# Sample value products of a decoder step with the probabilities stationary in column groups, and their rows turned by PE

## The chip, the cores and the metric

The kernel runs on one core of one Trainium2 chip. The metric is the device time of one execution in microseconds. It was timed three times; the figure used is the median. One more execution was taken with the hardware profiler, and every duration below is from it.

## The reference

One inference step of a hybrid decoder layer: 512 prompt tokens and, beside them, 8 sequences with 4 new tokens each (32 sample rows). The model width is 1024, all inputs are float32. What matters here is the sliding-window attention of the sample rows: 8 query heads over 2 key/value heads of 128 columns, a window of 128 cached keys per sequence, and the 4 new keys of the sequence itself.

```python
    qg = qb.reshape(B, N, Tq, N_KV, G, HD)
    s = jnp.einsum('bnqkgd,bnskd->bnkgqs', qg, kb).astype(jnp.float32) * (HD ** -0.5)
    ...
    s = jnp.where(valid[None, :, None, None], s + bias, -jnp.inf)
    sk = sink.astype(jnp.float32).reshape(1, 1, N_KV, G, 1, 1)
    m = jnp.maximum(jnp.max(s, axis=-1, keepdims=True), sk)
    p = jnp.exp(s - m)
    p = p / (jnp.sum(p, axis=-1, keepdims=True) + jnp.exp(sk - m))
    o = jnp.einsum('bnkgqs,bnskd->bnqkgd', p.astype(vb.dtype), vb)
    ...
        kk = jnp.concatenate([k_cache.astype(k.dtype), k], axis=1)
        vv = jnp.concatenate([v_cache.astype(v.dtype), v], axis=1)
```

The last `einsum`, probabilities times values, is the value product. Its result goes through an output projection (`w_attn_o`), is gated together with a recurrent branch, and a gated feed-forward layer follows.

## The kernel before, in words

All activations are kept with the model dimension on the partitions and the 544 rows (512 prompt, 32 sample) along the free axis, in two halves. The large matmuls split their float32 operands into a high and a low part and take three products (`hH` with `wh`, `hL` with `wh`, `hH` with `wl`). A projection `step` (L331) is 24 such matmuls over eight blocks of the model dimension for one half of the rows; `pmin` is its output tile for the input projection, `pmao` for the attention output projection, `pg` is the tile of the recurrent gates.

The order of the work is written by hand. A counter of ticks, `now`, goes forward by one with each step (`tick`, L194). Beside the steps run generators, entered by `start_at` with a tick (L183): when their tick has come, `sides` (L187) runs them up to their next `yield`, which means "go on at the next tick", and `yield 2` two ticks later. What a generator issues stands in each engine's queue between two steps. So a smaller number in the table of ticks moves a generator ahead of steps, and each `yield` between two parts puts one step of 24 matmuls between them.

The generator that the change touches is `sample_attn(g)` (L746), once for each of two groups `g` of four sequences, begun at tick `SAMPLE[g] - 3` (L925, the table in L74). Its parts, one tick apart unless said otherwise:

- the loads of the cached keys and values, 512 KB each, into two of the five buffers of the raw pool, on the DMA queue of SP (L750); the weights of the coming steps use the same pool;
- two ticks later eight transposes of the keys by PE into `pkc` (L760), and then their copies `kcT` by ACT (L765);
- the scores `pss` (L770 to L773): the queries against the new keys, then four products, each with the 32 queries of one sequence stationary, into 32 partitions of the output;
- the softmax in two parts, on DVE and ACT, in the tile `ss`;
- three transposes of the probabilities into `pst` (L783 to L785);
- two copies by DVE, `spt` (L788, L789), and the value product `pso` (L790 to L797). It keeps the new values `vnt` stationary first, with all 128 columns of the probabilities moving; then, for each of the four sequences and two key/value heads, it keeps the cached values stationary (128 keys by 128 columns) and moves 16 columns of the probabilities. A float32 matmul is two records in the trace, so the product has 2 + 16;
- eight copies by ACT, `aH`, and eight subtractions by DVE, `aL` (L799 to L804), of 16 columns per head. They put the result, as high and low part, into the columns of the sample rows of the tiles `A` that the output projection reads.

The result of `pso` thus has the value columns on its partitions and (sequence, head, token) along the free axis, as `A` wants it. PE's other side work at these ticks belongs to the prompt's attention: `psc` (scores), `pt` (transposed probabilities, L701), `pvp` (value products). PSUM tiles of side work come from one pool of five banks, and small SBUF tiles such as `spt` from one of ten.

Of the kernel before, what the change touches and what calls it, by code (L numbers as in the profile page):

```python
# [17 lines left out]
P = 128  # L18
# [11 lines left out]
NH = 8  # L30
NKV = 2
HD = 128
# [38 lines left out]
LAST_PLACES = {29: ('p3', 'p1', 'a22'), 30: ('p3', 'p1', 'a22'), 31: ('p1', 'a22')}  # L71
FIRST = 5
ATTN = (8, 10, 12, 14, 16, 18, 20, 22, 24, 27, 30, 33, 36, 39, 42, 45)
SAMPLE = (43, 47)  # L74
WARM = 18
GATES = (51, 53, 55, 57, 73, 74, 75, 76)
EXPS = (58, 59, 60, 61, 78, 79, 80, 81)
# [46 lines left out]
def hawk_step(ctx, tc, I, O):  # L124
    nc = tc.nc
    act, dve, pool, pe = nc.scalar, nc.vector, nc.gpsimd, nc.tensor
# [16 lines left out]
    def S(name, dt=F32):  # L143
        return sp.tile([P, SLOT], dt, tag="s", name=name)

    def T(name, dt=F32):
        return tp.tile([P, FLAT + 4], dt, tag="t", name=name)

    def RAW(name):
        return rp.tile([P, D], F32, tag="raw", name=name)  # L150
# [4 lines left out]
    def PX(name):  # L155
        return psx.tile([P, 512], F32, tag="aux", name=name)
# [4 lines left out]
    def f32(ap):  # L161
        return ap.bitcast(F32)

    def mm(out, l, r, start, stop):
        pe.matmul(out, l, r, start=start, stop=stop)  # L165

    def sub(out, a, b):
        dve.tensor_tensor(out=out, in0=a, in1=b, op=ALU.subtract)  # L168
# [7 lines left out]
    def stt(out, a, s_, b, op0, op1):  # L176
        dve.scalar_tensor_tensor(out=out, in0=a, scalar=s_, in1=b, op0=op0, op1=op1)  # L177
# [5 lines left out]
    def start_at(t, gen):  # L183
        serial[0] += 1
        side.append([t, serial[0], gen])
# [27 lines left out]
    ident = keep.tile([P, P], F32, name="ident")  # L213
# [184 lines left out]
    h = Full("h")  # L398
# [256 lines left out]
    def softmax_a(s3, nh, sink, nm):  # L655

        st = SM("st_" + nm, [P, 6, 2], "st")
        mx, ng, sm, dn, ex = (st[:, z, :nh] for z in range(5))
        dve.tensor_reduce(mx, s3, AX.X, ALU.max)
        dve.tensor_tensor(out=mx, in0=mx, in1=sink, op=ALU.max)  # L660
        dve.tensor_scalar(ng, mx, -1.0, None, ALU.mult)  # L661
        sub(dn, sink, mx)
        for j in range(nh):
            act.activation(s3[:, j, :], s3[:, j, :], AF.Exp, bias=ng[:, j:j + 1], accum_out=sm[:, j:j + 1])  # L664
        act.activation(ex, dn, AF.Exp)
        return sm, ex

    def softmax_b(s3, nh, sm, ex):
        add(sm, sm, ex)
        dve.reciprocal(sm, sm)  # L670
        for j in range(nh):
            dve.tensor_scalar(s3[:, j, :], s3[:, j, :], sm[:, j:j + 1], None, ALU.mult)
# [57 lines left out]
    vnt = cp.tile([NKV * NS, HD], F32, name="vnt")  # L730
# [15 lines left out]
    def sample_attn(g):  # L746
        raws, kcT = [], []
        for nme in ("cache_win_k", "cache_win_v"):
            t_ = RAW(f"{nme}{g}").rearrange("p (b x) -> p b x", b=4)
            nc.sync.dma_start(out=t_, in_=I[nme][0, 4 * g:4 * g + 4].rearrange("b j k d -> j b (k d)"))  # L750
            raws.append(t_)
        kraw, vraw = raws
        yield 2
        pxs = []
        for half in range(2):
            px = PX(f"pkc{g}{half}")
            for b in range(2):
                for kv in range(NKV):
                    c0 = (2 * b + kv) * P
                    pe.transpose(px[:, c0:c0 + P], kraw[:, 2 * half + b, kv * HD:(kv + 1) * HD], ident)  # L760
            pxs.append(px)
        yield
        for half in range(2):
            kt = S(f"kcT{g}{half}")
            act.activation(kt[:, 0:512], pxs[half], AF.Copy)  # L765
            kcT.append(kt)
        yield
        ps = PX(f"pss{g}")
        qg = qs[:, 4 * g:4 * g + 4, :, :].rearrange("p b h t -> p (b h t)")
        mm(ps[:, 2 * WIN:SKEY], qg, kn.rearrange("p k n -> p (k n)"), True, True)  # L770
        for b in range(4):
            mm(ps[32 * b:32 * b + 32, 0:2 * WIN], qs[:, 4 * g + b, :, :].rearrange("p h t -> p (h t)"),
               kcT[b // 2][:, (b % 2) * 256:(b % 2) * 256 + 256], True, True)  # L773
        yield
        s = T(f"ss{g}")
        stt(s[:, 0:SKEY], ps[:, 0:SKEY], SCALE, biasS[:, g, :], ALU.mult, ALU.add)
        s3 = s[:, 0:SKEY].rearrange("p (o j) -> p o j", o=1)
        se = softmax_a(s3, 1, sinkr, f"smp{g}")
        yield
        softmax_b(s3, 1, *se)  # L780
        yield
        px = PX(f"pst{g}")
        pe.transpose(px[:, 0:P], s[:, 0:P], ident)  # L783
        pe.transpose(px[:, P:2 * P], s[:, P:2 * P], ident)
        pe.transpose(px[:64, 2 * P:3 * P], s[:, 2 * P:SKEY], ident)  # L785
        yield
        pt = T(f"spt{g}")
        dve.tensor_copy(pt[:, 0:2 * P], px[:, 0:2 * P])  # L788
        dve.tensor_copy(pt[:64, 2 * P:3 * P], px[:64, 2 * P:3 * P])  # L789
        po = PX(f"pso{g}")  # L790
        o = po[:, 0:P]
        mm(o, vnt, pt[:64, 2 * P:3 * P], True, False)
        for b in range(4):
            for kv in range(NKV):
                c0 = b * 32 + kv * 16
                mm(o[:, c0:c0 + 16], vraw[:, b, kv * HD:(kv + 1) * HD],
                   pt[:, kv * P + c0:kv * P + c0 + 16], False, b == 3 and kv == NKV - 1)  # L797
        yield
        ov = o.rearrange("p (b h t) -> p b h t", b=4, h=NH)  # L799
        for hd in range(NH):  # L800
            oh, ol = (A.t[hd][z][:, SEQ + 16 * g:SEQ + 16 * g + 16].rearrange("p (b t) -> p b t", b=4)
                      for z in range(2))
            act.activation(oh, ov[:, :, hd, :], AF.Copy)
            sub(ol, ov[:, :, hd, :], f32(oh))  # L804
# [119 lines left out]
    for g in range(2):  # L924
        start_at(SAMPLE[g] - 3, sample_attn(g))  # L925
    for c in range(8):
# [808 lines left out]
    def ends(z):  # L1735
        ps = PM(f"pend{z}")
        o = ps[:, 0:256]
        for k in range(CH):
            wh, wl = (usplit["dl", k, 1][j].rearrange("p k n -> p (k n)")[:, 256 * z:256 * z + 256]
                      for j in range(2))  # L1740
            fh, fl = (F.t[QL * CH + k][j][:, P:2 * P] for j in range(2))
            pe.matmul(o, fh, wh, start=k == 0, stop=False, skip_group_check=True)
            if k == 0:
                for j in range(2):
                    pe.matmul(ps[:, j * P:(j + 1) * P], ft[4 + 2 * z + j][:, P:2 * P], ident, start=False, stop=False,
                              skip_group_check=True)
            pe.matmul(o, fl, wh, start=False, stop=False, skip_group_check=True)
            pe.matmul(o, fh, wl, start=False, stop=k == CH - 1, skip_group_check=True)
        return o
# [43 lines left out]
    o = ends(0)  # L1793
# [4 lines left out]
    o = ends(1)  # L1798
# [46 lines left out]
```

## Time and profile before

| | us |
|---|---|
| timed runs | 1009.07, 1008.91, 1009.62 |
| median | 1009.07 |
| profiled execution | 1010.02 |
| its span (first to last instruction) | 1008.1 |
| granted TensorE clock, mean | 0.995 |
| PE busy | 995.6 |
| DVE busy | 731.6 |
| ACT busy | 579.8 |

The span is what the profile covers; 1.9 us of the profiled execution lie around it. PE is the engine of the matmuls and transposes, PEld its loads of the stationary operand, DVE and ACT are the vector and the scalar engine, POOL is GpSimd, and SP issues DMAs. The granted clock is the share of full speed that TensorE was given. A row of the chain of waits has a start, a length, and the work that the end of the program depended on in that time.

### The profile page before, as it was taken

The numbers are of one execution on the slowest core, as the hardware profiler recorded it, in microseconds if no ns is written. First come the engines' busy times: TensorE is split into PE (matmuls) and PEld (weight loads), VectorE is DVE, ScalarE is ACT, GpSimd is POOL, SyncE is SP. The second block draws the span as 40 slices with busy tenths as digits, with TensorE's granted clock in tenths as the row PEclk, the third lists the DMA queues.
The fourth block names the chain that finished last, engine by engine and source line by source line (L and its number), as shares of the span: only waits on it lengthen the run. The fifth ranks groups of instructions, "written<-read, shape, count | busy, mean of one in ns | idle before, by whom it ended". The sixth has DMA issues, their size and how long they took to land.

```text
span 1008.1 us, 20186 instructions
## 1 busy us (share of the span) xinstructions
PE 995.6 (99%) x7835; PEld 985.3 (98%) x7835; DVE 731.6 (73%) x1553; ACT 579.8 (58%) x1422; POOL 151.5 (15%) x270
## 2 busy tenths in 40 slices
PE   8999999999999999999999999999999999999997
PEld 7999999999999999999999999999999999999996
DVE  6476688444945655489787687878888888887865
ACT  6444554458448634556776656565656565656662
POOL 3131010001403432020000111111111111110004
PEclk9999999989999999999999999999999999999999
DMA  7743222322323245317235858585858676767712
GB/s 210 229 149 92 63 85 86 105 85 68 111 74 105 86 138 144 109 44 239 79 91 137 181 136 179 137 189 130 191 126 191 126 189 135 179 147 178 215 45 89
DMA packets 207687, 133.40 MB, mean 132 GB/s; under 512 B 6546, under 2 KB 194306, under 8 KB 207560
## 3 DMA queue, kind: packets, MB, share of 16 engines
q1 hardware_dynamic: 197944, 112.20, 39.2%
q0 software_dynamic: 9600, 17.90, 11.3%
q10 hardware_dynamic: 48, 2.03, 0.5%
q8 instruction: 61, 1.00, 0.4%
q14 instruction: 34, 0.28, 0.1%
HBM read 111.82 MB, written 9.14 MB: 120 GB/s over the span
## 4 chain that ended last, share of the span: by engine, by line
PE 93%; DVE 3%; DMA 2%; ACT 2%; issue 0%; SPq 0%; ACTq 0%; DVEq 0%
PE pmin L165 22%; PE pmdn L165 17%; PE pux L1396 15%; PE puy L1396 7%; PE pq L1396 6%; PE pmout L165 5%; PE pmao L165 5%; PE pmlo L165 4%; PE puz L1396 4%; PE pg L165 1%; PE psc L165 1%; PE pvp L165 1%; DMA raw_up_s<-in_w_up_dram 1%; DMA raw_in<-in_w_in_dram 1%; PE pt L701 1%; PE ptok L165 1%
## 5 line engine op out<-in xcount | busy, mean ns | idle before, releaser
L165 PE MATMUL pmin<-hH,wh_in 128*128 128x256 f32 (+1 forms) x576 | 168.0, 294 | 0.0
L165 PE MATMUL pmin<-hH,wl_in 128*128 128x256 f32 (+1 forms) x576 | 165.6, 290 | 0.0
L165 PE MATMUL pmin<-hL,wh_in 128*128 128x256 f32 (+1 forms) x576 | 165.5, 289 | 0.0
L165 PE MATMUL pmdn<-fH,wh_dn 128*128 128x256 f32 (+1 forms) x448 | 129.2, 288 | 0.2 <-DVE ft L174 0.2
L165 PE MATMUL pmdn<-fH,wl_dn 128*128 128x256 f32 (+1 forms) x448 | 129.2, 288 | 0.2 <-DVE wl_dn L168 0.2
L165 PE MATMUL pmdn<-fL,wh_dn 128*128 128x256 f32 (+1 forms) x448 | 129.1, 288 | 0.0
L177 DVE SCALAR_TENSOR_TENSOR uc<-u,fv,uc 128x560 f32<-128x560 f32 x128 | 102.0, 797 | 13.3 <-ACT uc L1427 13.2
L165 PEld LDWEIGHTS pmin<-hH,wh_in 128*128 128x128 f32 x576 | 109.2, 190 | 1.7 <-issue 0.6
L165 PEld LDWEIGHTS pmin<-hL,wh_in 128*128 128x128 f32 x576 | 109.2, 191 | 0.0
L165 PEld LDWEIGHTS pmin<-hH,wl_in 128*128 128x128 f32 x576 | 108.8, 190 | 0.0
L165 PEld LDWEIGHTS pmdn<-fH,wh_dn 128*128 128x128 f32 x448 | 84.3, 188 | 0.6 <-issue 0.6
L165 PEld LDWEIGHTS pmdn<-fH,wl_dn 128*128 128x128 f32 x448 | 84.4, 188 | 0.4 <-DVE wl_dn L168 0.4
L165 PEld LDWEIGHTS pmdn<-fL,wh_dn 128*128 128x128 f32 x448 | 84.3, 188 | 0.0
L1522 ACT COPY u<-pux 128x272 f32<-128x272 f32 x52 | 20.1, 386 | 85.4 <-PE pux L1396 85.3
L168 DVE TENSOR_TENSOR u<-puy,u 128x240 f32<-128x240 f32 (+2 forms) x78 | 24.6, 344 | 49.8 <-PE puy L1396 32.5
L174 DVE TENSOR_TENSOR ft<-ft,pmdn 128x256 f32<-128x256 f32 (+1 forms) x104 | 45.2, 435 | 16.6 <-PE pmdn L165 16.0
L277 ACT ACTIVATE wh_in<-raw_in 128x512 fp32r<-128x512 f32 x72 | 44.2, 628 | 20.8 <-PE pmin L165 10.4
L282 DVE TENSOR_TENSOR wl_in<-raw_in,wh_in 128x512 fp32r<-128x512 f32 x72 | 48.2, 683 | 1.6 <-ACT wh_in L277 1.5
L1427 ACT ACTIVATE uc<-u,fv 128x560 f32<-128x560 f32 x64 | 48.2, 755 | 0.0
L664 ACT ACTIVATE s<-s,st 128x256 f32<-128x256 f32 (+1 forms) x32 | 15.2, 476 | 50.7 <-DVE st L661 43.3
L168 DVE TENSOR_TENSOR wl_dn<-raw_dn,wh_dn 128x512 fp32r<-128x512 f32 x56 | 38.3, 685 | 0.0
L1322 POOL DMA_DIRECT2D raw_up_s<-raw_up_s x26 | 22.7, 872 | 101.7 <-issue 5.2
(773 smaller groups left out, 3415.7 us busy)
## 6 DMA issues: line engine op xcount, KB each, us to landing
raw_in<-in_w_in_dram SPq DMA_DIRECT2D x36, 512.0 KB
raw_dn<-in_w_down_dram SPq DMA_DIRECT2D x56, 256.0 KB
raw_up_s<-in_w_up_dram SPq DMA_DIRECT2D x26, 512.0 KB
raw_up_s<-raw_up_s POOLq DMA_DIRECT2D x26, 256.0 KB, 6.1
raw_ao<-in_w_attn_o_dram SPq DMA_DIRECT2D x8, 512.0 KB
raw_lo<-in_w_lru_o_dram SPq DMA_DIRECT2D x8, 512.0 KB
raw_out<-in_w_out_dram SPq DMA_DIRECT2D x8, 512.0 KB
x1d<-x SPq DMA_DIRECT2D x8, 272.0 KB
```

What stands on the lines that cost most here:

```text
L165: pe.matmul(out, l, r, start=start, stop=stop)
L168: dve.tensor_tensor(out=out, in0=a, in1=b, op=ALU.subtract)
L174: dve.tensor_tensor(out=out, in0=a, in1=b, op=ALU.add)
L177: dve.scalar_tensor_tensor(out=out, in0=a, scalar=s_, in1=b, op0=op0, op1=op1)
L277: act.activation(hl[0], raw, AF.Copy)
L282: (eng or dve).tensor_tensor(out=hl[1], in0=raw, in1=f32(hl[0]), op=ALU.subtract)
L664: act.activation(s3[:, j, :], s3[:, j, :], AF.Exp, bias=ng[:, j:j + 1], accum_out=sm[:, j:j + 1])
L701: pe.transpose(pt[:, (2 * ch + j) * P:(2 * ch + j + 1) * P], s3[:, j, ch * P:(ch + 1) * P], ident)
L1322: pool.dma_start(out=w["p4"], in_=w["p2"], accum_op=ALU.add)
L1396: pe.matmul(ps[:, :HN], w, x, start=start and k == 0 and i == 0, stop=stop and k == 3 and i == 2, skip_group_check=True)
L1427: act.activation(yt[j][:, 0:FLATU], u[:, 0:FLATU], AF.Copy, scale=fv[:, j:j + 1])
L1522: act.copy(e[nm_], z)
```

## The change

The product keeps the probabilities stationary and moves the values. First the 64 rows for the new keys: all 128 probability columns stationary, `vnt` moving. Then, with the key/value head as the outer loop and the sequence as the inner one, 32 probability columns of one sequence stationary, and 128 value columns moving, into 32 partitions of the output. (The probabilities of the heads that belong to the other key/value head are zero in these columns, as they were laid out before.) The result now has (sequence, head, token) on its partitions and the value columns along the free axis. So it is copied to SBUF by DVE (`so`), transposed by PE into a tile `psot` of its own one tick later, and one tick after that the eight copies and eight subtractions read `psot`. To make room for the two ticks, `SAMPLE` goes from (43, 47) to (41, 46): group 0 begins two ticks earlier, group 1 one.

```diff
-SAMPLE = (43, 47)
+SAMPLE = (41, 46)
...
         po = PX(f"pso{g}")
-        o = po[:, 0:P]
-        mm(o, vnt, pt[:64, 2 * P:3 * P], True, False)
-        for b in range(4):
-            for kv in range(NKV):
-                c0 = b * 32 + kv * 16
-                mm(o[:, c0:c0 + 16], vraw[:, b, kv * HD:(kv + 1) * HD],
-                   pt[:, kv * P + c0:kv * P + c0 + 16], False, b == 3 and kv == NKV - 1)
-        yield
-        ov = o.rearrange("p (b h t) -> p b h t", b=4, h=NH)
+        mm(po[:, 0:HD], pt[:64, 2 * P:3 * P], vnt, True, False)
+        for kv in range(NKV):
+            for b in range(4):
+                mm(po[32 * b:32 * b + 32, 0:HD], pt[:, kv * P + 32 * b:kv * P + 32 * b + 32],
+                   vraw[:, b, kv * HD:(kv + 1) * HD], False, kv == NKV - 1)
+        yield
+        so = T(f"so{g}")[:, 0:HD]
+        dve.tensor_copy(so, po[:, 0:HD])
+        yield
+        px = PX(f"psot{g}")
+        pe.transpose(px[:, 0:P], so, ident)
+        yield
+        ov = px[:, 0:P].rearrange("p (b h t) -> p b h t", b=4, h=NH)
         for hd in range(NH):
```

On PE, the product of group 0 stands behind a prompt block's transposes `pt` now, and the scores `pss` of group 1 follow it directly (before):

```order
L165 MATMUL pmin_1_2761<-hH_175,wh_in_2565 128x288
L165 MATMUL pmin_1_2761<-hL_176,wh_in_2565 128x288
L165 MATMUL pmin_1_2761<-hH_175,wl_in_2566 128x288
L701 MATMUL pt_3_2789<-ident,s_3_2684 128x128 x4
L165 MATMUL pso_2797<-spt_2794,vnt 128x128
L165 MATMUL pso_2797<-spt_2794,cache_win_v_2376 128x16 x8
L165 MATMUL pss_2807<-kn,qs 128x64
L165 MATMUL pss_2807<-kcT_2755,qs 32x256 x2
L165 MATMUL pss_2807<-kcT_2757,qs 32x256 x2
L165 MATMUL pmin_0_2816<-hH_161,wh_in_2618 128x256
```

In the changed kernel it stands two steps earlier and alone between two projection steps:

```order
L165 MATMUL pmin_1_2669<-hH_175,wh_in_2470 128x288
L165 MATMUL pmin_1_2669<-hL_176,wh_in_2470 128x288
L165 MATMUL pmin_1_2669<-hH_175,wl_in_2471 128x288
L165 MATMUL pso_2714<-vnt,spt_2711 128x128
L165 MATMUL pso_2714<-cache_win_v_2275,spt_2711 32x128 x8
L165 MATMUL pmin_0_2731<-hH_161,wh_in_2527 128x256
```

The eight products are now 32 partitions by 128 columns where they were 128 by 16, and the scores of group 1 have another place, a step later. Two steps behind the product, the same queue in the changed kernel holds the turn of its rows:

```order
L165 MATMUL pmin_1_2782<-hH_175,wl_in_2585 128x288
L701 MATMUL pt_3_2810<-ident,s_3_2701 128x128 x4
L801 MATMUL psot_2815<-ident,so_2772 128x128
L165 MATMUL pmin_0_2829<-hH_161,wh_in_2630 128x256
L165 MATMUL pmin_0_2829<-hL_162,wh_in_2630 128x256
```

It has moved to where the product itself stood before, behind the transposes `pt` of the last prompt block. On DVE, the copies `spt` that the product waits for stand behind the first part of that block's softmax (`s`, `st`) in the changed kernel, and the copy `so` behind its second part:

```order
L168 TENSOR_TENSOR tL_2_2698<-pt_2_2641,tH_2_2697 128x512
L177 TENSOR_SCALAR s_3_2701<-psc_3_2646,btab_1714 128x512
L659 TENSOR_REDUCE st_3_2703<-s_3_2701 128x2
L660 TENSOR_TENSOR st_3_2703<-st_3_2703,sinkb 128x2
L661 TENSOR_SCALAR st_3_2703<-st_3_2703 128x2
L168 TENSOR_TENSOR st_3_2703<-sinkb,st_3_2703 128x2
L788 COPY spt_2711<-pst_2653 128x256
L789 COPY spt_2711<-pst_2653 64x128
L282 TENSOR_TENSOR wl_in_2695<-raw_in_2423,wh_in_2694 128x512
L174 TENSOR_TENSOR st_3_2703<-st_3_2703 128x2
L670 RECIPROCAL st_3_2703<-st_3_2703 128x2
L672 TENSOR_SCALAR s_3_2701<-s_3_2701,st_3_2703 128x256 x2
```

Before, the copies came after both parts of that softmax, with one split of weights (`wl_wg`) between (before):

```order
L672 TENSOR_SCALAR s_3_2684<-s_3_2684,st_3_2686 128x256 x2
L282 TENSOR_TENSOR wl_wg_2738<-raw_wg_2514,wh_wg_2737 128x512
L788 COPY spt_2794<-pst_2751 128x256
L789 COPY spt_2794<-pst_2751 64x128
L282 TENSOR_TENSOR wl_wg_2787<-raw_wg_2514,wh_wg_2786 128x512
```

They have moved ahead of the second part; on the DMA queue of SP, the loads of group 0's cached keys and values have moved ahead of one weight load.

## The prediction

> **What bounds the kernel now.** I read the page first: its busy times, its row of granted clocks and its chain that ended last.
>
> ```profile
> PE 995.6 (99%) x7835; PEld 985.3 (98%) x7835; DVE 731.6 (73%) x1553; ACT 579.8 (58%) x1422; POOL 151.5 (15%) x270
> PEclk9999999989999999999999999999999999999999
> PE 93%; DVE 3%; DMA 2%; ACT 2%; issue 0%; SPq 0%; ACTq 0%; DVEq 0%
> ```
>
> PE works 99% of the span and is 93% of the chain, so a microsecond taken from PE's queue is a microsecond off the end, as long as nothing that PE waits for becomes late. DVE has a quarter of the span free. The clock row has one digit that is not a 9: slice 8, which at 25.2 us a slice (a fortieth of the span of 1008.1) is 201.6 to 226.8 us. That is where the sample groups' value products stand. So the next view is the chain of waits there (start, length, tile, instructions).
>
> ```profile
> 182.50 3.02 PE pmin L165 x24
> ...
> 186.67 3.20 PE pmin L165 x24
> 189.87 0.87 PE pkc L760 x8
> 190.74 2.83 PE pmin L165 x24
> ...
> 198.26 2.30 PE pso L165 x18
> ...
> 201.40 7.75 PE pmin L165 x48
> ...
> 216.20 2.30 PE pso L165 x18
> 218.50 2.60 PE pg L165 x12
> 221.10 6.61 PE pmin L165 x48
> 227.71 1.58 PE pg L165 x12
> 229.29 6.03 PE pmin L165 x48
> ```
>
> Two things cost time. Each value product `pso` takes 2.30 us of PE for 18 records. And behind each, work of known length is longer than elsewhere: 48 `pmin` matmuls 7.75 us against 6.03 (at 229.29), 12 `pg` 2.60 against 1.58, the next 48 `pmin` 6.61. The excess is 7.75 - 6.03 = 1.72 and (2.60 - 1.58) + (6.61 - 6.03) = 1.60 us, 3.32 us together. The table by windows says what it is (length, then busy time of PE, PEld, DVE, ACT, POOL with counts, granted clock, DMA share, GB/s).
>
> ```profile
> 7.25:10.67 3.42, 1.40 (x12) 1.19 (x11) 2.69 (x11) 1.85 (x6) 0.00 (x0) 1.00 1.19 315
> 10.67:14.08 3.41, 2.86 (x14) 2.86 (x15) 3.16 (x8) 2.63 (x6) 2.73 (x14) 0.50 1.09 318
> 198.41:201.82 3.41, 3.41 (x32) 2.81 (x32) 1.19 (x4) 1.10 (x4) 0.00 (x0) 1.00 0.13 40
> 201.82:205.23 3.41, 3.41 (x19) 3.41 (x18) 2.06 (x11) 0.92 (x5) 0.00 (x0) 0.50 0.52 150
> 215.48:218.89 3.41, 3.41 (x28) 3.12 (x27) 0.14 (x1) 0.18 (x1) 0.00 (x0) 1.00 0.49 148
> 218.89:222.30 3.41, 3.41 (x17) 3.41 (x16) 1.26 (x8) 1.89 (x9) 0.00 (x0) 0.50 0.51 154
> 1000.55:1003.96 3.41, 1.64 (x16) 1.27 (x13) 2.17 (x8) 2.93 (x7) 0.00 (x0) 1.00 0.79 296
> 1003.96:1007.37 3.41, 0.00 (x0) 0.00 (x0) 0.00 (x0) 0.00 (x0) 0.00 (x0) 1.00 0.79 276
> ```
>
> The clock stands at 0.50 for exactly 3.41 us after each product. The two closings begin five windows of 3.41 us apart and 56 windows after the one at 10.67, so the windows lie on one grid. At the start a window with 1.40 us of PE work is followed by half clock; near the end one with 1.64 us leaves the next at 1.00. The windows ahead of the two closings in the middle show PE busy throughout, so busy records alone don't explain them. But most of that busy time is `pso`:
>
> ```profile
> 198.41:201.82 3.41, 2.16 (x18) 1.94 (x17) 0.50 (x3) 0.55 (x3) 1.00 0.13 40
> 215.48:218.89 3.41, 2.37 (x18) 2.16 (x18) 0.14 (x1) 0.18 (x1) 1.00 0.49 148
> L165 PE MATMUL pso<-spt,cache_win_v x32: 262/262/283, 198.6 to 218.2; 128*128 128x16 f32 x32
> ```
>
> Leaving `pso` out, the windows hold 3.41 - 2.16 = 1.25 and 3.41 - 2.37 = 1.04 us of PE work, both below 1.40. In `pso` itself PE mostly loads: each record of the last row brings a 128x128 block of weights and then moves 16 columns. I take it that such loads don't count as work for whatever grants the clock, and that the two closings are the price of this shape. The 3.32 us is about half of the 6.82 us spent at half clock.
>
> **The change part by part.**
>
> *The product.* Out go 16 records of 16 moving columns per group; in come 16 records with 32 stationary and 128 moving columns, spread over four column groups. The nearest rows are the scores `pss`, which have that shape with 256 columns and eight records, and the old product's first part (start, length, columns).
>
> ```profile
> 181.60 0.33 PE L165 MATMUL pss<-kn,qs 128*128 128x64 f32 x2
> 181.86 0.64 PE L165 MATMUL pss<-kcT,qs 128*32 128x256 f32 x8
> 182.43 0.39 PE L165 MATMUL pmin<-hH,wh_in 128*128 128x256 f32 x1
> ...
> 198.19 0.48 PE L165 MATMUL pso<-spt,vnt 64*128 64x128 f32 x2
> 198.61 1.96 PE L165 MATMUL pso<-spt,cache_win_v 128*128 128x16 f32 x16
> ```
>
> The four score products take 182.43 - 181.86 = 0.57 us from start to the next start: two records of 256 columns in each of four groups, side by side. The new product has four records of 128 columns per group, the same columns per group, so 0.57 us. Its first part keeps 128 moving columns on a 64-row, 128-column array: 198.61 - 198.19 = 0.42 us as now. Going back to full-width matmuls costs something: the 24 `pmin` behind `pss` take 3.02 us against 2.83, so 0.19. Sum 0.42 + 0.57 + 0.19 = 1.18, about 1.2 us. Its lower bound is 0.83 (0.26 us, the pitch of the scores' own first part from 181.60 to 181.86, plus 0.57); its upper bound 2.2, if the 18 records followed each other at some 0.12 us, the pitch of the 256-column `pmin` (2.83 / 24). I take 1.2, since `pss` has all but the number of columns in common.
>
> The Trainium skill bears on the third term ("TensorEngine Tiling (Array Packing)", Key Properties): changing the tiling mode drains TensorE. The rows agree with the 0.19 us that stands in the sum already; the new product changes mode as often as `pss` does, once in and once out, and the drain on the way in is inside the 0.57.
>
> *The turn.* One transpose more per group, `psot`, costs what one of the eight `pkc` transposes costs: 0.87 / 8 = 0.11 us.
>
> *Beside PE.* The new copy `so` (128x128 out of PSUM) lies between the `spt` copies below, 0.27 to 0.42 us each, on DVE, a whole projection step of about 3 us ahead of its transpose; it is hidden. Without that cover it would cost its 0.3 us each. The eight `aH` and eight `aL` read `psot` instead of `pso`, otherwise unchanged; the projection that reads them stands behind the 48 `pmin` of 229.29, over 15 us after the second product.
>
> *The move.* Group 0's loads start two ticks earlier, group 1's one. Its cached keys and values stand one weight load earlier on SP; the load that takes the values' place in the raw pool waits, as now, until `pso` has read them, and `pso` comes earlier too. The tightest wait is that of group 0's product for the probabilities: `pst` will stand directly behind `psc`, whose end is the start of the `pmin` at 186.67, and DVE works on that score block first.
>
> ```profile
> 189.25 0.15 DVE L168 TENSOR_TENSOR st<-sinkb,st 128x2 f32<-128x2 f32 x1
> ...
> 194.66 0.42 DVE L788 COPY spt<-pst 128x256 f32<-128x256 f32 x1 [2.45 <-PE pst L785]
> 195.00 0.27 DVE L789 COPY spt<-pst 64x128 f32<-64x128 f32 x1
> ```
>
> The copies can begin at 189.40 in the old clock and end 0.6 us later, at 190.0. PE reaches the product after three `pst` (0.32), eight `pkc` (0.87) and 24 `pmin` (3.2), at 191.1. That leaves 1.0 us of slack, where now there are 2.9 (195.27 to 198.19). I count nothing for it, and one microsecond in a rival.
>
> *The clock.* With a product of 1.2 us, a window that holds it whole still has 3.41 - 1.2 = 2.2 us of other PE work, above the 1.64 that left the clock at 1.00. So both closings go: -3.3 us. They come back if the product takes more than 3.41 - 1.64 = 1.77 us and doesn't count as work.
>
> *Sum.* Per group 1.18 + 0.11 - 2.30 = -1.0, for two -2.0; the clock -3.3; together **-5.3 us**. The profiled execution took 1010.02 us (span 1008.1 and 1.9 around it), 0.95 above the median of the three timed runs, 1009.07. Taken off the profiled execution the sum gives 1004.7, off the median 1003.8. I can't see whether the 0.95 is the cost of profiling or something of that execution alone, so I go between the two: **1004.2**.
>
> **The rivals.**
>
> *The closings have another cause.* PE's records say busy for 3.41 of 3.41 us; if the gate follows something that the change leaves alone (the place in the program, say), the 3.3 stays and only 2.0 goes: 1010.0 - 2.0 = 1008.0, or 1007.0 off the median. For it: busy time is what a profile shows. Against it: only these two windows of the whole middle are followed by half clock, and only they are mostly `pso`. The Trainium skill ("TensorE: Matmul & The Clock Gate", Part 1) states that the clock drops to half after at least one idle window of about 3.4 us; it gives the same window length and the same half, but by its words neither window here, with PE busy, should have closed the gate at all. Chance 10%.
>
> *One closing goes, or comes and goes.* Where the products fall on the grid may differ between executions, so the timed runs may already have been spared one now and then. With 1.7 us less gain: 1005.7 to 1006.4. Against it: three runs lie within 0.71 us, less than one closing. Chance 8%.
>
> *A wait takes the place.* PE stands before group 0's product for `spt` when DVE's block is late by over 1.0 us, or before a weight step because the load behind the cached values comes late. A microsecond or two: 1005 to 1007. Chance 6%.
>
> *Slower: the column groups run one after another.* If each of the 16 records cost its whole duration as the row has it for 256 columns, 0.39 us, and a 128-column record 0.27, the product would take 0.42 + 16 x 0.27 = 4.7 us for 2.30: +2.4 per group, +0.2 for the turns, and the closings would stay: about 1015.
>
> ```profile
> L165 PE MATMUL pss<-kcT,qs x16: 379/391/403, 181.9 to 201.0; 128*32 128x256 f32 x16
> ```
>
> With the closings kept, it is slower than before from a product of about 2.2 us. Against it: eight such records start within 0.57 us, so they overlap. Only the reading of one column group by four records in a row, not two, is new. Chance 4%.
>
> That leaves 72% for the forecast, whose own range is 1003.0 to 1005.6: half a microsecond for either start of the sum, and 0.35 us per group down, with a little more up, for the product. To hold eight in ten, the range goes up over a single closing, a wait and the first rival as far as **1008.0**; low is **1003.0**. With about 2 us (0.2%) as what a measurement of this kernel tells from no change, faster means under 1007.05: the forecast, one closing, most of the waits, and a little of the first rival: 0.87. Same, up to 1011.1: most of the first rival, 0.09. Slower: 0.04.
>
> **What would show it.** The granted clock at 1.00 in every window from 195 to 230; The `pmin` behind both products at 2.8 to 3.2 us per 24, the `pg` at 1.6 per 12; `pso` at 1.2 us in the chain of waits and `psot` at 0.11. No idle PE ahead of `pso` or of the `pmin` step behind it. Wrong would be: half clock after a product of 1.2 us (then the loads were not the cause), 16 records at a pitch of 0.1 us or more, or a wait of PE for `spt`, `so` or a weight split.

## The result, and the profile after

Six executions of the changed kernel took 1002.55 to 1003.93 us, median **1002.90**; six of the kernel before, among them the three shown above, 1005.94 to 1009.87, median 1008.99. The ratio is 0.9946 (0.9934 to 0.9957). The forecast was 1004.2 with a range from 1003.0, so the median lies a tenth of a microsecond below the range. A second set gave 1003.83 (five executions) beside 1006.91 (nine of before), ratio 0.9963 (0.9949 to 0.9977). Over everything measured here the kernel before has 70 executions in four sets, 1005.94 to 1011.65 with a mean of 1008.1, and the changed one 11 in the two sets above, 1002.55 to 1005.07 with a mean of 1003.5: **4.6 us** less (on the means of the two sets alone, 5.4 and 3.5). The profiled execution took 1003.73 us, 6.29 less than that of before.

The page of the changed kernel, granted clock and engines:

```profile
PE 988.9 (99%) x7837; PEld 978.5 (98%) x7837; DVE 732.0 (73%) x1555; ACT 579.4 (58%) x1422; POOL 151.0 (15%) x270
PEclk9999999999999999999999999999999999999999
```

The 8 in slice 8 is gone. The chain of waits at the same place in the work (start, length, tile, instructions):

```profile
187.74 3.20 PE pmin L165 x24
190.94 0.99 PE pso L165 x18
191.93 3.03 PE pmin L165 x24
...
199.81 0.44 PE pt L701 x4
200.25 0.11 PE psot L801
200.36 6.00 PE pmin L165 x48
...
210.22 0.99 PE pso L165 x18
211.21 3.39 PE pmin L165 x24
214.60 1.58 PE pg L165 x12
216.18 2.86 PE pmin L165 x24
219.04 0.11 PE psot L801
```

Each product takes 0.99 us, and the step behind it 0.20 more than a step of 24 that follows full-width work (3.03 against 2.83, 3.39 against 3.18 to 3.21): 1.19 us where 1.18 were forecast. The turn is 0.11. The `pg` and the 48 `pmin` have their full speed. PE's timeline around the first product (start, length) and its two kinds of record:

```profile
190.87 0.48 PE L165 MATMUL pso<-vnt,spt 64*128 64x128 f32 x2
191.28 0.64 PE L165 MATMUL pso<-cache_win_v,spt 128*32 128x128 f32 x16
191.86 0.38 PE L165 MATMUL pmin<-hH,wh_in 128*128 128x256 f32 x1
```

From start to start 191.86 - 191.28 = 0.58 us for 16 records, 0.57 forecast: four groups work side by side, as they do in the scores. On DVE the tight wait is visible:

```profile
188.81 0.15 DVE L168 TENSOR_TENSOR st<-sinkb,st 128x2 f32<-128x2 f32 x1
188.88 0.42 DVE L788 COPY spt<-pst 128x256 f32<-128x256 f32 x1
189.22 0.27 DVE L789 COPY spt<-pst 64x128 f32<-64x128 f32 x1
...
192.06 0.29 DVE L798 COPY so<-pso 128x128 f32<-128x128 f32 x1 [0.89 <-PE pso L165]
```

The copies end at 189.49, and the product starts at 190.87: 1.4 us to spare (1.0 forecast). At the second product, which the prediction left out, it is less: the copies end at 209.35 and the product starts at 210.15, 0.8 us later. `so` lies wholly beside the next step.

Up to the first `pmao`, which starts at 231.53 instead of 236.90, the profiled executions differ by 5.37 us, for 5.3 forecast (0.13 of it is there already at 26 us, before anything that the change touches). The other 0.9 of the 6.29 comes later in small pieces in work that the change does not touch, such as a load of the prompt that PE waits for (4.50 us instead of 4.76); no experiment bears on them.

### The profile page after: what moved, and what is told of

Same layout as the page of the kernel before. It is cut to its first block, busy times and chain, and to the rows that moved or that the text cites. A ratio compares the mean times of both kernels' runs of the same rounds, so it can differ in the third digit from the quotient of the medians.

```text
span 1002.0 us, 20195 instructions
## 1 busy us (share of the span) xinstructions
PE 988.9 (99%) x7837; PEld 978.5 (98%) x7837; DVE 732.0 (73%) x1555; ACT 579.4 (58%) x1422; POOL 151.0 (15%) x270
## 4 chain that ended last, share of the span: by engine, by line
PE 92%; DVE 3%; ACT 2%; DMA 2%; issue 0%; SPq 0%; ACTq 0%; DVEq 0%
PE pmin L165 22%; PE pmdn L165 16%; PE pux L1400 15%; PE puy L1400 7%; PE pq L1400 6%; PE pmout L165 5%; PE pmao L165 5%; PE pmlo L165 4%; PE puz L1400 4%; PE pg L165 1%; PE psc L165 1%; PE pvp L165 1%; DMA raw_up_s<-in_w_up_dram 1%; DMA raw_in<-in_w_in_dram 1%; PE pt L701 1%; PE ptok L165 1%
```

## The experiments

The gate is here whatever grants TensorE its clock. A closing is a window of 3.41 us at half clock, and the grid is the row of such windows, one behind the other, on which the half clock begins and ends.

**Theory.** The old product closes the gate by its shape: a window of 3.41 us that holds all of it moves too few columns. **Rivals.** The gate follows the place in the program, the number of loads or records, or something else that the change moved along.

### The move alone

```diff
-SAMPLE = (43, 47)
+SAMPLE = (41, 46)
```

> The kernel before with the new table alone: SAMPLE = (41, 46), the product as it was. Theory (the old product's shape closes the clock gate, and the new product is 1.1 us shorter): two products of 2.30 us remain and one window of half clock behind each wherever a window holds most of one; 1007 to 1010 us, ratio 0.998 to 1.001. Rival (the gate closes because of the place in the program, not because of the product): closings go or move apart from the products, about 1005.7 us.

Ten executions: 1005.61 to 1006.75 six times, 1007.19, and 1008.76 to 1009.45 three times; median 1006.49, ratio 0.9991 (0.9979 to 1.0003). The move gives no gain clear of noise. Six of the ten lie below the 1007 to 1010 us of the theory, nearer the rival's 1005.7, and the profiled execution, at 1006.11 us, had no closing in the middle:

```profile
191.15 2.31 PE pso L165 x18
193.45 2.92 PE pmin L165 x24
...
211.52 2.30 PE pso L165 x18
213.82 3.28 PE pmin L165 x24
```

The products are as long as ever, and what follows them has full speed. The grid explains it. In this execution its edges, followed from the one half-clock window at the start (12.18 to 15.59), are at 193.08 and at 213.56: each product is cut by one. In before's profile each lay in one window, but for the first 0.15 us of one. The distance between the two products is 20.37 us, 5.97 windows, so both are cut or neither; hence two levels some 3 us apart. The granted clock on record for each execution agrees: 0.993 in the three long ones, 0.997 in the seven others, and two windows of 3.41 us at half clock are 0.0034 of the span. In before the distance is 17.94 us, 5.26 windows, so none, one or both can close, and its 70 executions spread over 5.7 us without such a gap; of the 64 with a clock on record, the 18 above 1009 us had 0.993 to 0.996, the 18 under 1007 us 0.996 to 1.000. **The closings come and go with the phase of the grid**, which differs from execution to execution: the half clock at the start begins at 10.68 us in before, 11.93 in after, 12.18 here.

### The product in two halves

```diff
         for b in range(4):
+            if b == 2:
+                yield
             for kv in range(NKV):
```

> The kernel before with each product cut in two by one tick: two sequences, then a projection step of about 3 us, then the other two. Every instruction stays. Theory (a window of 3.41 us with about 1.8 us of loads for 16 moving columns reads as too little work): no window holds more than 0.9 us of them, so no half clock behind either product and 48 pmin at 6.0 us; 3.3 us less than before where before has both closings, about 1005.5 us, ratio 0.9967. Rival (the gate follows the place, or the count of these records): unchanged, 1009 us.

Median 1006.75 of twelve, ratio 0.9985 (0.9975 to 0.9995). The profile (1005.40 us) has no half clock anywhere before the end:

```profile
197.68 1.41 PE pso L165 x10
199.08 0.83 PE pss L165 x10
199.92 3.03 PE pmin L165 x24
202.95 0.80 PE pso L165 x8
```

Eleven of the twelve are at most 1007.16 us; one, 1008.68, is as long as a closing would make it, but its granted clock is 0.998, inside what the other eleven have (0.996 to 1.000): something else made it long. The expected 1005.5 is what its fastest executions reach; the gain against before's median is smaller because before does not always pay for two closings.

### 32 moving columns

```diff
-                c0 = b * 32 + kv * 16
-                mm(o[:, c0:c0 + 16], vraw[:, b, kv * HD:(kv + 1) * HD],
-                   pt[:, kv * P + c0:kv * P + c0 + 16], False, b == 3 and kv == NKV - 1)
+                c0 = b * 32
+                mm(o[:, c0:c0 + 32], vraw[:, b, kv * HD:(kv + 1) * HD],
+                   pt[:, kv * P + c0:kv * P + c0 + 32], False, b == 3 and kv == NKV - 1)
```

> The kernel before with 32 moving columns per product where it had 16: the 16 columns of the other heads hold zeros, so the sum is the same. Records and loads stay as many. If the load of 128x128 sets the pitch, 16 records still take 1.8 us. Theory (the gate counts columns that move): the columns in the window double; if that is enough, no half clock and about 1005.7 us, if the threshold lies higher still, 1009 us with half clock behind both. Rival (it counts loads, records or busy time): half clock behind both, 1009 us.

```profile
198.50 2.32 PE pso L165 x18
200.81 0.82 PE pss L165 x10
201.63 6.22 PE pmin L165 x48
```

The product is 0.02 us longer for twice the columns. Twelve executions lie between 1005.79 and 1007.56 us, median 1006.79, mean 1006.75; before, on the same chip, had 35 from 1006.45 to 1010.48, mean 1008.15. The upper end is gone, 1.4 us on the mean. In the profiled execution an edge cut both products, so the profile itself says nothing of what 32 columns do in a whole window; the probes below do.

### The old records behind the new product

```diff
                    vraw[:, b, kv * HD:(kv + 1) * HD], False, kv == NKV - 1)
+        for b in range(4):
+            for kv in range(NKV):
+                c0 = b * 32 + kv * 16
+                mm(po[:, P + c0:P + c0 + 16], vraw[:, b, kv * HD:(kv + 1) * HD],
+                   pt[:, kv * P + c0:kv * P + c0 + 16], True, True)
```

> The changed kernel with the sixteen records of the old shape (cached values stationary, 16 columns moving) issued once more behind each new product, into unused columns of its PSUM tile, read by nobody. Theory: 1.8 us more per group for the records, 1.0 to 1.3 us per group with the switch into and out of column groups, and half clock again behind both: 1003 + 3.6 + 3.3 = 1010 us. Rival (the closings went with the place): 1003 + 3.6 = 1006.5 us with the clock at 1.00.

A miss: 1007.45 us (1006.45 to 1008.41, ten executions), about the records alone, and no level 3 us above. The records take their time (`pso` is 2.88 us instead of 0.99), but the closings did not come back, so the theory in its first form, "nearly all of the 1.9 us in a window", was too simple: either other work in the window counts closely, or products that are begun and ended one by one differ from accumulating ones. The probes tell these apart.

### Probes: many stretches in one execution

Dead stretches (operands `qs`, results read by nobody) between projection steps of the changed kernel, 13 of one kind at ticks 59 to 71 and 10 of another from tick 79, in two generators of this form:

```diff
+    def probe_a():
+        for i in range(13):
+            po = PX(f"pra{i}")
+            mm(po[:, 0:P], qf[:64, P:2 * P], qf[:64, 0:P], True, False)
+            for c0 in range(0, P, 16):
+                mm(po[:, c0:c0 + 16], qf[:, 0:P], qf[:, P + c0:P + c0 + 16], False, c0 == P - 16)
+            yield
```

> The changed kernel with 23 added stretches of dead work that nobody reads, each between two projection steps of about 3 us. The first 13 have the old product's shape (one product of 128 moving columns, then 16 records of 16 moving columns that accumulate); the last 10 have the 16 records alone, each product begun and ended by itself, as in the run before this one that repeated the old product. They fall on the 3.41 us grid at ever new places. Theory (a window that holds nearly all of the 1.9 us closes the gate): about 45% of either kind, some 6 of 13 and 4 or 5 of 10, are followed by a window at half clock, and the content of the window, not its place, divides them, between 1.6 and 1.9 us. Rival (products that are begun and ended by themselves don't close it, which would explain the clock of the run that repeated the old product): some 6 of 13 and 0 of 10. Rival (place alone): none of either.

Six of the 13 were followed by half clock, none of the 10. The table by windows, on this execution's grid (length, busy times, granted clock, DMA), and the stretch's own share of two of them:

```profile
252.79:256.20 3.41, 3.41 (x28) 3.29 (x29) 2.23 (x3) 0.00 (x0) 0.25 (x2) 1.00 0.33 93
256.20:259.62 3.42, 3.42 (x27) 3.13 (x25) 1.29 (x2) 2.47 (x5) 1.74 (x2) 1.00 0.22 65
314.23:317.64 3.41, 3.41 (x28) 3.16 (x28) 1.02 (x2) 0.00 (x0) 0.00 (x0) 1.00 0.20 60
317.64:321.06 3.42, 3.42 (x17) 3.42 (x16) 0.75 (x1) 1.20 (x2) 0.00 (x0) 0.50 0.31 94
```

```profile
252.79:256.20 3.41, 2.22 (x18) 2.00 (x18) 1.00 0.33 93
314.23:317.64 3.41, 2.37 (x18) 2.16 (x18) 1.00 0.20 60
```

The first stretch begins 0.09 us ahead of its window and leaves 3.41 - 2.22 = 1.19 us to full-width projection matmuls: no closing. The second lies whole in its window and leaves 1.04: half clock in the next. So it is for all 13: the six that lay whole in one window closed it, the seven that an edge cut did not. Both windows show PE busy for 3.41 of 3.41 us, so busy time does not tell. The ten shorter stretches take 1.69 us in the chain of waits and leave 1.7, so that no phase tests them; what the rival about begun and ended products says of them had to wait for the third probe.

With 32 columns in the 13, and 24 column-group products (1.86 us) in the 10:

> The same with other shapes: 13 stretches with 32 moving columns in place of 16, at the same records and the same pitch, and 10 in the new product's shape but three times as many column-group products, so that they last about 2 us. Theory (the gate counts columns that move): with 32 columns few or none of 13 close it, as no run with 32 columns in the product went over 1007.6 us; of the column-group stretches none, although their windows hold as little other work. Rival (the gate counts loads or records, or other work in the window): as with 16 columns, about 6 of 13 and 4 of 10.

None of the 13 and none of the 10; this execution has no half clock at all before its end. The stretches fell otherwise on the grid than those with 16 columns: three of the 13 (beginning at 252.67, 279.92 and 306.83 in the chain of waits) lay whole in one window. A window that held a whole stretch of 32 columns, the one behind it, and the stretch's share:

```profile
252.08:255.49 3.41, 3.41 (x29) 3.15 (x28) 2.28 (x3) 0.00 (x0) 0.93 (x2) 1.00 0.15 39
255.49:258.91 3.42, 3.42 (x26) 3.13 (x24) 0.62 (x2) 1.95 (x4) 1.06 (x1) 1.00 0.41 119
```

```profile
252.08:255.49 3.41, 2.39 (x18) 2.16 (x18) 1.00 0.15 39
```

As much PE time, the same records and loads as with 16 columns, 1.02 us left over, and the clock stays, in all three windows of this kind; with 16 columns it fell in all six. That rules out loads, records and busy time as what the gate counts; of what was varied here, the moving columns are left. The column-group stretches left 1.5 us and so proved nothing; the third probe made them longer (`range(8)` rounds of four products, 2.30 us), and the begun-and-ended ones too (22 records):

> Again dead stretches between projection steps of the changed kernel, longer. 13 in column groups: one product of 128 moving columns, then 32 column-group products of 128 moving columns, about 2.3 us, so that as little other work (1.1 us) is left in a window as with the old product. 10 with 22 records of 16 moving columns, each product begun and ended by itself, about 2.4 us, where 16 such records (1.7 us) closed nothing. Theory (a window closes the gate when it leaves less than some 1.2 us for work that moves columns): none of the 13, since column-group products move columns all the time; 2 to 4 of the 10 (the share of places where 2.4 us lie whole in a window is 1.0 / 3.4, and somewhat more with an end cut off). Rival (any long stretch that is not a full-width projection step closes it): 3 to 5 of the 13. Rival (only accumulating products close it): 0 of the 10.

None of the 13, and five of the 10. The windows, with those of 16 columns from 351.82 on:

```profile
263.07:266.48 3.41, 3.41 (x75) 2.96 (x75) 1.02 (x2) 0.00 (x0) 0.00 (x0) 1.00 0.17 49
266.48:269.90 3.42, 3.42 (x38) 3.14 (x40) 1.30 (x4) 2.37 (x5) 0.56 (x1) 1.00 0.35 105
351.82:355.23 3.41, 3.41 (x32) 3.41 (x32) 1.34 (x1) 0.38 (x1) 0.18 (x1) 1.00 0.52 152
355.23:358.64 3.41, 3.41 (x16) 3.41 (x16) 0.00 (x0) 0.59 (x2) 0.00 (x0) 0.50 0.00 0
365.47:368.88 3.41, 3.41 (x31) 3.41 (x31) 0.00 (x0) 0.29 (x1) 0.00 (x0) 1.00 0.52 152
368.88:372.30 3.42, 3.42 (x30) 3.42 (x30) 1.40 (x3) 3.00 (x7) 1.07 (x1) 1.00 0.02 5
```

A column-group stretch that lies whole in its window (first row) leaves the clock at 1.00, and so do the three others that lie whole in one: the new shape counts as work. Begun-and-ended products do close the gate once they are long enough, so that rival falls. Three of these stretches in the chain of waits (start, length):

```profile
352.91 2.36 PE prb L165 x22
...
365.34 2.36 PE prb L165 x22
...
397.42 2.36 PE prb L165 x22
```

The first leaves 1.09 us of its window ahead of it and closes. The second lies in its window from 365.47 on, for 2.23 us, leaves 1.18, and does not; nor does the third, cut by an edge at 399.60, which leaves 1.23. A stretch of the first probe (2.30 us in the chain) leaves 1.11 when it lies whole in a window, and closes. **Counted by the chain, the line lies between 1.11 and 1.18 us** of full-width projection work beside 16-column records in a window. The busy times of the stretches shown further up come out 0.07 to 0.16 us longer where a stretch lies whole, since their first records begin before the work ahead of them has ended; by that count the closed windows of these two probes leave 0.89 to 1.04 us and the open ones 1.07 or more. Either count parts the closed windows from the open ones; only the figure differs. The repeated old records above left more than that, or shared their window with 0.99 us of the new product, which now counts; that the theory gave them 3.3 us was the error.

### What the changed form is worth, and two additions

The changed kernel once more, on a chip with the kernel before and the next one:

> The changed kernel once more, beside the one before, for the size of the effect over many executions. If the closings in the kernel before come and go with the phase of the grid (none, one or two, each 1.7 us), the kernel before spreads over some 4 us, the changed one over 1.5 us, the medians lie about 5 us apart (ratio 0.995), less than the 6.1 us of the first six runs. If both closings are there in most executions, the medians stay 6 us apart (0.994).

1003.83 us beside 1006.91, ratio 0.9963 (0.9949 to 0.9977): medians 3.1 us apart, less than either value expected. The spreads are 1.9 and 3.3 us. Its profiled execution, the longest of the five with 1005.07 us, shows one thing that makes an execution long still: half clock at the start, two windows of it.

```profile
6.89:10.30 3.41, 1.58 (x14) 1.37 (x12) 2.97 (x13) 1.38 (x4) 0.00 (x0) 1.00 1.17 314
10.30:13.71 3.41, 2.67 (x13) 2.68 (x14) 2.63 (x6) 2.63 (x7) 2.23 (x16) 0.50 1.09 331
13.71:17.13 3.42, 3.42 (x18) 3.42 (x17) 3.39 (x8) 3.42 (x9) 0.03 (x1) 0.50 1.22 274
```

The product for the new keys in column groups too:

```diff
-        mm(po[:, 0:HD], pt[:64, 2 * P:3 * P], vnt, True, False)
+        for b in range(4):
+            mm(po[32 * b:32 * b + 32, 0:HD], pt[:64, 2 * P + 32 * b:2 * P + 32 * b + 32], vnt, True, False)
```

> The changed kernel with the product for the new keys in four column groups as well: four times 32 probability columns stationary over 64 rows, the new values moving into 32 partitions each, in place of one product with all 128 columns. If the first part's 0.42 us is what one full-width product of 128 columns takes by itself, four side by side take about 0.15 to 0.3: 0.1 to 0.25 us less per group, 1002.5 us, ratio to the changed kernel 0.9995. Rival (64 rows are another mode than 128, and each change of mode costs 0.2 us): no gain, 1003 us.

```profile
190.97 0.93 PE pso L165 x24
```

0.06 us less per product, where 0.1 to 0.25 were expected: four side by side are hardly quicker than one at full width. The median of 1002.71 us is lower than the 1003.83 beside it by more than that explains; its profile has one half-clock window at the start, not two.

The old table with the new product:

```diff
-SAMPLE = (41, 46)
+SAMPLE = (43, 47)
```

> The changed kernel with the old table, SAMPLE = (43, 47): the new product and the turn without the earlier start. Theory (the move only makes room, and no wait hangs on it): the same time as the changed kernel, 1003 us, since the last aH and aL then come at tick 55, and the projection that reads them starts later still. Rival (the turn comes too late for that projection, or two groups' side work collides): 0.5 to 2 us more, with idle PE ahead of pmao.

1004.78 us (1004.07 to 1006.92, twelve executions), ratio to before 0.9971 (0.9959 to 0.9982), with a mean of 1005.0, 1.6 us above the changed kernel's 11 executions. But the changed kernel did not run beside it, and its ratios of 0.9946 and 0.9963 have intervals (0.9934 to 0.9957, 0.9949 to 0.9977) of which the second overlaps this one, so the size of the loss is not shown. The profile shows a wait, as the rival had it, but in another place, ahead of the second product:

```profile
PE pso L165 <- DVE spt L789: 0.8, 1, 0.8
```

PE comes to the second product some 2.6 us earlier than in the kernel before, with nothing lost to closings and a shorter first product, and DVE begins to copy the probabilities 0.4 us later (213.48 for 213.05), behind the eight `aL` of group 0's turned rows. So the earlier start is worth these 0.8 us in the profiled execution.

Ten more dead matmuls at the start, in the kernel before and in the changed one (the latter with the new keys in column groups):

```diff
     pe.transpose(ps0[:, 0:8], rows_a[0:8, :], ident[0:8, 0:8])
+    for z in range(10):
+        mm(pw[:, (z % 4) * P:(z % 4 + 1) * P], ones, ident, True, True)
```

> The kernel before with ten more dead matmuls at the very start, into the tile of those that are there already, while PE waits for the first input. They leave no window at the start with little work. Theory: no half clock at 10 to 18 us, and what is left of the spread between executions is the value products' own closings: three levels, none, one and two, 1.7 us apart, about 1005.5, 1007.2 and 1008.9 us, and a median about 1 us below the kernel before. Rival (the spread comes from elsewhere, DMA or launch): the spread stays a smooth 4 us.

1005.54 us (1003.63 to 1006.13, nine executions), ratio 0.9967 (0.9955 to 0.9979): 2.4 us less on the median, where about 1 was expected. The start runs at full clock. Three levels did not show: nothing near 1008.9, and the profiled execution, at 1004.93 with no closing at either product (an edge cuts both), is 1.3 us above the fastest. So the rest of the spread is not the products' closings alone, and nine executions are too few to say how much of it is.

> The changed kernel with the product for the new keys in column groups (0.06 us less per group in the run before) and with the ten dead matmuls at the start. Theory: the half-clock window at the start, one or two windows in three of four profiles of this form, goes, for 0.5 to 1.5 us; about 1001.8 us, and a spread below 1 us. Rival (the added matmuls delay the transposes behind them): 1003 us or more.

**1001.63 us** (1001.15 to 1002.75, six executions), ratio to the kernel before 0.9934 (0.9918 to 0.9950): the fastest form here. The spread of 1.6 us is above the 1 us expected.

## Why the prediction was right, and where it was mis-sized

- *The product* (1.18 us): right, 1.19, and by the terms it was added up from: 0.41, 0.58 and 0.20 for 0.42, 0.57 and 0.19. The scores, with half as many records and the same columns per group, were the right row to read it from.
- *The turn, the copy, the move*: right, 0.11 us and hidden. The slack was 1.4 us, not 1.0, and the tightest place is the second product with 0.8, not the first, as the prediction had it. The run with the old table shows that the slack was worth watching: without the earlier start it is gone there.
- *The clock*: the mechanism was right (records that move 16 columns per load count for too little, column groups count as work), the size was not. The step "both closings go: -3.3 us" took the profiled execution for every execution. Between the two profiled ones it holds, 5.37 us up to `pmao` for 5.3. But the kernel before pays for none, one or two. On the means, the 4.6 us less 2.0 for the instructions leave 2.6 for the clock; the run with 32 columns, which takes away closings and nothing else, gained 1.4 on the mean. The granted clocks on record, which count the half clock at the start and the end in, give a third estimate: 0.9961 on the mean of 64 executions of before, 0.9977 of 11 of after, and 0.0016 of a span of 1005 us is 1.6 us. So the term is **1.4 to 2.6 us on average**, most likely near the lower end, not 3.3; the first set alone (5.4 less 2.0) would have 3.4, and the few executions make it no sharper. With a clock term near 1.5 about 1 us of the 4.6 has no account: the profiled pair, too, differs by 0.9 us behind `pmao`.
- *The rival that a closing "goes, or comes and goes"* was told in its own words and given 8%. It is what the 70 executions show. The argument against it, three runs within 0.71 us, was weak: they happened to be at the upper end. The Trainium skill ("TensorE: Matmul & The Clock Gate", Part 1) says of the 3.4 us window that it is free-running and doesn't start anew with the kernel. The runs agree (10.68, 11.93 and 12.18 us for the half clock at the start), and by that sentence the phase of one profile should not have been taken for all.
- That the median still came out at 1002.9, below the sum, has two parts: the first six executions of before lay high (median 1008.99, over all 70 it is 1007.8), and those of after were, with 1002.9, half a microsecond below the median of all 11, 1003.4. The total was right partly by that luck.
- *The first rival*, another cause of the closings, falls: of 13 stretches of the old shape elsewhere in the program, all six that lay whole in a window closed it. The same section of the Trainium skill has the clock drop after an idle window. Here windows in which PE is busy 3.41 of 3.41 us were followed by half clock; the measurement decides.
- *The bound for the gate* was set at 1.64 us of other work; the probes put it between 1.11 and 1.18, counted by the chain. Before's own first window closed with 1.25 us besides `pso`, of which 0.83 are the scores `pss`; that these count for less than a projection step is argued, not shown.

## What to carry to other kernels

Matmuls that load 128 columns of weights to move 16 cost twice here: 32 moving columns took no longer than 16 (2.32 us for 2.30 per product), so the moving side does not set the pitch, and where a row of them took 2.3 us of one window of 3.41 us, the next window ran at half clock. Widening the moving side to 32 columns, cutting the row in two, or making the small operand stationary in column groups avoided the second cost in these runs; the last one lowered the first too (0.99 us for 2.30). A profile is one phase of the gate's grid: look at several executions before a closing that it shows is priced into every run.

## What the runs showed of the hardware that was not expected

- The gate is sharp: beside 16-column records, a window with 1.11 us or less of full-width work (counted by the chain of waits) was followed by half clock in all eleven cases of the first and third probe, and one with 1.18 us or more in none.
- Twice the moving columns at the same pitch (2.32 us for 2.30) was enough to keep the clock, in three windows that held a whole stretch.
- Four products of 64 rows side by side in column groups take 0.35 us from start to start (190.90 to 191.25), one at full width 0.41 (190.87 to 191.28): why they gain so little stays open.
